# Splitting and moving small pieces around the attention of a two-layer decoder trunk, and cutting GpSimd's MLP tiles in halves

## The chip, the core and the metric

The kernel runs on one core of one Trainium2 chip. The metric is the device time of one execution, in microseconds. Five engines work side by side, each on its own list of instructions: PE multiplies matrices, DVE and ACT are the two wide elementwise engines, POOL (GpSimd) is a third, slower one, and SP issues the DMAs. PE's clock has two levels, 1.2 and 2.4 GHz; the profile shows it as a granted share, 0.50 and 1.00, and something between where a window holds both.

## What is computed

One sequence of 1024 tokens and width 1024 goes through two layers, all in float32:

```python
h = x
h = h + gla_mix(rmsnorm(h), ...)                  # layer 0: chunked gated linear attention, 4 heads
h = h + conv_ffn(rmsnorm(h), ...)                 # MLP0, hidden 2816, causal conv of width 3
k, v = shared_kv(h, ...)                          # one K/V projection, rotary on k
h = h + diff_attn(rmsnorm(h), k, v, ...)          # layer 1: 8 heads, 128 values each, causal
h = h + conv_ffn(rmsnorm(h), ...)                 # MLP1
return rmsnorm(h)

# diff_attn, per head: two score maps of 64 features each
a = softmax(q1 @ k1.T) - lam * softmax(q2 @ k2.T)
o = rmsnorm(a @ v) * (1 - lam_init)               # per head and token
# conv_ffn
u = h @ w_in ; c = conv3(u) ; a, g = split(c) ; out = (silu(g) * a) @ w_out
```

## The kernel before

Features lie on the 128 partitions and the 1024 tokens along a tile, in eight tiles of features. A float32 operand is split into a hi part (`xh`, `wh`, and the first half of `wp`, `xp`, `rp`, `lp`), which ACT copies with rounding, and a lo part (`xl`, `wl`, the second half), which is the operand less its hi part. A product is three matmuls, hi by hi, hi by lo, lo by hi. The lo part is mostly made by DVE (`lo_of`, a `scalar_tensor_tensor`, line 117), in some places by POOL (`tt`, line 114). `fine` (line 314) cuts an operation of 1024 columns on POOL into four of 256; on DVE it leaves it whole.

**The MLPs** use a scheme with seven products of half size in place of eight, so sums and differences of quarters are needed. Of the weights these are `sums`, `pieces` and `pieces_by_form` (lines 215 to 250): POOL makes them in 128x512 tiles, and `halves` (line 205) splits each result into `wp`. `mid` (line 855) adds the products (`u`) and `mix` (line 948) makes the sums of the hidden tiles (`c` to `mt`), both in part on POOL. `Wide.factor0` (line 401) scales a tile of the normalized stream and splits it with `halves` into `xp`; it is called eight times ahead of each MLP, half of them for the quarter "11", half for "21".

**Attention** (from line 1245) first projects and rotates. `rope_unit` (line 1260) projects k or q of a head for half of the tokens; after the second half it sends `xsb` through a DMA that swaps partitions, into `xw`. `rope_end` finishes the rotation in the next unit (`xw` by `sinr`, then `y` plus `xw`) and puts the rotated tile in a list, which the next call stores to DRAM, `kd` or `qd` (line 1253). `Attn.load` (line 1293) reads it again into `st`, and `qk_split` splits it. For head 0 the table `todo` (line 1477) names after which of the projection units this happens.

Then a loop runs over 64 steps (8 heads of 8 blocks of 128 queries), with the parts of several blocks in flight: scores (line 1332), maximum (`mx`), exponentials (`e`, line 1350), combination of both maps, transposes (`tp`, line 1378), hi and lo of the transposed weights (`ah` on ACT, `al` on DVE), and the products with v (`pv`, lines 1392 to 1394). A list `fill` hangs other work onto the steps: the projections of the later heads until step 46, the last `rope_end`, loads (`osr`) and splits of finished heads, loads of the residual `h`, and from step 48 on the units of the output product (`wo_unit`, line 1440, tile `dwo`). `finish` (line 1415) normalizes a head's output `osb`: PE spreads `ro` over the partitions (`rb`, line 311), DVE multiplies. The last head's output is split whole and completes the last W_o units. `wo_unit` adds to `h`, and `Late.add` sums the squares (`ssq`) that `begin` (line 389) multiplies by ones.

PE, ACT and SP run in the order in which the program is written. DVE's and POOL's order is made by a scheduler when the program is built.

Of the kernel before, what the change touches and what calls it, by code (L numbers as in the profile page):

```python
# [50 lines left out]
def trunk(  # L51
# [153 lines left out]
    def halves(x, name, eng=None):  # L205

        t = U(name, F32R)
        ACT.activation(t[:, H(0)], x, AF.Copy)  # L208
        if eng is POOL:
            tt(POOL, t[:, H(1)], x, t[:, H(0)].bitcast(F32), ALU.subtract)  # L210
        else:
            lo_of(DVE, t[:, H(1)], x, t[:, H(0)])
        return t

    def sums(ra, rg):

        tmp = U("wt")
        a11, a12, a21, a22 = ra[:, H(0)], ra[:, H(1)], rg[:, H(0)], rg[:, H(1)]
        s1, s2 = tmp[:, H(0)], tmp[:, H(1)]
        tt(POOL, s1, a21, a22, ALU.add)  # L220
        tt(POOL, s2, s1, a11, ALU.subtract)
        tt(POOL, a21, a11, a21, ALU.subtract)
        return a11, a12, a21, a22, s1, s2

    def pieces(ra, rg):


        a11, a12, s3, a22, s1, s2 = sums(ra, rg)
        yield halves(a11, "wp")
        yield halves(s2, "wp")  # L230
        tt(POOL, s2, a12, s2, ALU.subtract)
        yield halves(a12, "wp")
        yield halves(s3, "wp")
        yield halves(s1, "wp")
        yield halves(a22, "wp")
        pair.clear()
        yield halves(s2, "wp")

    def pieces_by_form(*raws):
# [6 lines left out]
        for a11, a12, s3, a22, s1, s2 in xs:  # L246
            tt(POOL, a12, a12, s2, ALU.subtract)
        for q in (1, 4, 5, 2, 3):
# [65 lines left out]
    def fine(eng, o, a, b, op):  # L314

        for c in range(0, 1024, 256 if eng is POOL else 1024):
            q = slice(c, c + 256 if eng is POOL else 1024)
            tt(eng, o[:, q], a[:, q], b[:, q], op)
# [46 lines left out]
    class Wide:  # L365
# [35 lines left out]
        def factor0(self, d):  # L401

            self.f["11" if d < ND // 2 else "21"].append(halves(self.scaled(d, 0), "xp"))

# [443 lines left out]
    def ffn(l, nm, g):  # L848
# [6 lines left out]
        def mid(i, n, o):  # L855
# [3 lines left out]
            if i < 2:  # L859
# [9 lines left out]
                elif n == 1:  # L869
                    tt(DVE, g1, o, g1, ALU.add)  # L870
                    tt(POOL, a2, a2, g1, ALU.add)
                elif n == 3:
                    tt(DVE, g1, o, g1, ALU.add)
                    tt(POOL, g2, g2, g1, ALU.add)
                else:
                    tt(DVE, g1, o, g1, ALU.add)
# [71 lines left out]
        def mix(i):  # L948
# [4 lines left out]
            t, u = U("mt"), U("mt")  # L953
            tt(POOL, t[:, H(0)], b12, b11, ALU.subtract)
            tt(POOL, t[:, H(1)], b22, t[:, H(0)], ALU.subtract)
            tt(POOL, b12, b22, b12, ALU.subtract)
            tt(POOL, u[:, H(0)], b21, t[:, H(1)], ALU.subtract)
            if i == NF - 1:
# [288 lines left out]

    rp, tails, stores = {}, deque(), deque()

    def rope_end(eng=None):  # L1250
# [3 lines left out]
        while tails:  # L1254
            dst, y, xw = tails.popleft()
            fine(eng, xw, xw, sinr, ALU.mult)
            fine(eng, y, y, xw, ALU.add)
            stores.append((dst, y))

# [20 lines left out]
    def kq_units(hh):  # L1280
        return [(rope_unit, dst, sc, hf, part) for dst, sc in ((kd[hh], 1.0), (qd[hh], HD ** -0.5))
                for hf in range(2) for part in range(2)]

    class Attn:
# [8 lines left out]
        def load(self, j):  # L1293

            r = rawtile("st")
            self.raw[j] = r
# [118 lines left out]
        def finish(self):  # L1415
            for hf in range(2):
                stt(DVE, self.osb[:, H(hf)], self.osb[:, H(hf)], sub_w, bcast_rows(self.ro, H(hf)), ALU.mult, ALU.mult)

    osp = [dram.tile([P, S], F32, name=f"osp{i}") for i in range(AH - 2)]
    h, on, wdo = {}, [], {}  # L1420
# [15 lines left out]

    def o_split():
        on.append(split(osr.popleft(), eng=OE))

    def wo_unit(g, d, hf, ks=range(4)):  # L1440
# [25 lines left out]
        if hf == 1:  # L1466
# [5 lines left out]
    steps = AH * NB  # L1472
    OE = POOL
    KQE, OL, OS, RS, WOB, RE = 46, 45, 46, 47, 48, DVE
    AHEAD, LOADS = 1, 2
    heads = {0: Attn(0)}
    todo = {0: [(heads[0].load, 2)], 6: [(heads[0].load, 1)], 9: [(heads[0].qk_split, 1), (heads[0].v_split,)],
            10: [(heads[0].load, 0)], 13: [(heads[0].qk_split, 0)]}
    SIDE = DVE
# [13 lines left out]

    spread([u for a in range(2, AH) for u in kq_units(a)], -2, KQE)
    fill[KQE + 1].append((rope_end, RE))
    fill[KQE + 1].append((rope_end,))
    spread([(o_load, q) for q in range(4)], OL, OL + 1)
    spread([(o_split,) for q in range(4)], OS, OS + 1)
    fill[RS] += [(residual, d) for d in DORD]
    spread([(o_load, q) for q in (4, 5)], steps - 4, steps - 3)  # L1500
    spread([(wo_unit, 0, d, hf) for d in DORD for hf in range(2)], WOB, steps - 1)

    for s in range(-2, steps + 5):
        a, i = divmod(s + 2, NB)
# [42 lines left out]
        if 0 <= s - 4 < steps:  # L1547
            b, j = divmod(s - 4, NB)
            if j == NB - 1:
                hd = heads.pop(b)  # L1550
                hd.finish()
                if b < AH - 2:
                    nc.sync.dma_start(osp[b], hd.osb)
                elif b == AH - 2:
                    last = [split(hd.osb, eng=POOL)]
                else:
                    last.append(split(hd.osb))
        if s == steps - 1:
# [4 lines left out]
        if steps <= s < steps + 3:  # L1563
            for d in DORD[2 * (s - steps):2 * (s - steps) + 2]:
                wo_unit(1, d, 0, range(3))
    on.append(last[1])
# [112 lines left out]
```

## Time and profile before

| | |
|---|---|
| median of three runs | 2384.3 us (2382.56 to 2384.98) |
| the profiled execution's own time | 2386.05 us |
| its span | 2384.3 us |
| PE busy | 2323.3 us (97%) |
| DVE busy | 1823.3 us (76%) |
| ACT busy | 1041.2 us (44%) |
| POOL busy | 710.2 us (30%) |

By the trace, MLP0 runs from about 447 to 1085 us, the first projections of the attention from 1200, its heads from 1240 to 1656, the last units of W_o to about 1703, and MLP1 follows. A row of a time-ordered view gives start, duration, engine, line, operation, the tile written and those read, the shape, and in brackets how long the engine stood idle before and what it waited for. Adjacent equal operations stand in one row with their count (x2); durations of pipelined rows overlap a little.

### The profile page before, as it was taken

What the parts mean: (1) busy time and instruction counts of PE and PEld (TensorE: products, weight loads), DVE (VectorE), ACT (ScalarE), POOL (GpSimd) and SP (SyncE); (2) the same over time, 40 slices, a digit from 0 to 9 for tenths busy, and PEclk for the clock granted to TensorE, in tenths of its full rate; (3) what the DMA queues carried; (4) which work ended last, traced back from release to release, by engine and by line L of the source; (5) the groups of instructions that cost most, each with busy time, mean ns of one, the idle gap of its engine ahead of it and who ended that gap; (6) DMA issues with size and microseconds to landing.
All of it is one profiled execution on the core that took longest, in us unless ns stands there. A gap on an engine that the chain in (4) does not pass through costs nothing. (4 is left out here: it accounts for less than half of the span.)

```text
span 2384.3 us, 29798 instructions
## 1 busy us (share of the span) xinstructions
PE 2323.3 (97%) x10954; PEld 1884.4 (79%) x10954; DVE 1823.3 (76%) x2605; ACT 1041.2 (44%) x1865; POOL 710.2 (30%) x718
## 2 busy tenths in 40 slices
PE   9999999999999999999999999899999999999997
PEld 7878887777888888888877888777767888888886
DVE  6554554799999999867147877666799999999865
ACT  5433352344333444544125555543353433344553
POOL 0210101055545430000005655622046544441001
PEclk9999999999999999999999999999999999999998
DMA  5012134122323347324243333512213323248423
GB/s 185 1 53 71 54 109 161 43 84 88 112 102 105 106 186 278 119 75 176 82 141 114 112 110 116 182 67 92 76 45 115 124 84 115 84 147 305 145 84 102
DMA packets 101427, 271.25 MB, mean 114 GB/s; under 512 B 10272, under 2 KB 23200, under 8 KB 101280
## 3 DMA queue, kind: packets, MB, share of 16 engines
q1 hardware_dynamic: 101280, 269.34, 33.6%
q8 instruction: 86, 1.41, 0.2%
q14 instruction: 61, 0.50, 0.1%
HBM read 184.89 MB, written 76.02 MB: 109 GB/s over the span
## 5 line engine op out<-in xcount | busy, mean ns | idle before, releaser
L908 PE MATMUL pf<-xp,wp 128*128 128x512 f32 x1232 | 488.8, 397 | 12.8 <-DVE wp L117 12.7
L907 PE MATMUL pf<-xp,wp 128*128 128x512 f32 x1232 | 488.3, 396 | 1.5 <-ACT xp L208 1.3
L909 PE MATMUL pf<-xp,wp 128*128 128x512 f32 x1232 | 487.8, 396 | 1.7 <-DVE xp L117 1.5
L908 PEld LDWEIGHTS pf<-xp,wp 128*128 128x128 f32 x1232 | 232.3, 189 | 73.3 <-DVE wp L117 19.5
L907 PEld LDWEIGHTS pf<-xp,wp 128*128 128x128 f32 x1232 | 232.1, 188 | 59.1 <-ACT xp L208 3.3
L909 PEld LDWEIGHTS pf<-xp,wp 128*128 128x128 f32 x1232 | 232.1, 188 | 59.0 <-DVE xp L117 5.5
L1016 PE MATMUL out<-rp,lp 128*128 128x512 f32 (+1 forms) x632 | 247.0, 391 | 1.5 <-ACT rp L208 1.5
L1018 PE MATMUL out<-rp,lp 128*128 128x512 f32 (+1 forms) x632 | 246.6, 390 | 0.0
L117 DVE SCALAR_TENSOR_TENSOR c<-u,cv,c 128x1024 f32<-128x1024 f32 x176 | 246.4, 1402 | 0.0
L1017 PE MATMUL out<-rp,lp 128*128 128x512 f32 (+1 forms) x632 | 246.2, 390 | 0.0
L117 DVE SCALAR_TENSOR_TENSOR wp<-raw,wp 128x512 fp32r<-128x512 f32 x180 | 202.7, 1135 | 13.5 <-ACT wp L208 13.2
L114 DVE TENSOR_TENSOR u<-pf,u 128x512 f32<-128x512 f32 x300 | 200.4, 680 | 15.1 <-PE pf L909 10.1
L278 PE MATMUL pf<-xh,wh 128*128 128x512 f32 x458 | 186.3, 407 | 1.1 <-ACT wh L198 1.1
L114 POOL TENSOR_TENSOR rs_y<-rs_m,nhalf 128x4 f32<-128x4 f32 (+2 forms) x26 | 31.4, 1207 | 517.0 <-DVE rs_m L294 487.0
L279 PE MATMUL pf<-xh,wl 128*128 128x512 f32 x458 | 181.1, 395 | 0.8 <-DVE wl L117 0.8
L280 PE MATMUL pf<-xl,wh 128*128 128x512 f32 x458 | 181.1, 395 | 0.0
L934 ACT ACTIVATE c<-c 128x1024 f32<-128x1024 f32 x44 | 46.7, 1062 | 268.4 <-DVE c L117 268.4
L117 DVE SCALAR_TENSOR_TENSOR wp<-wt,wp 128x512 fp32r<-128x512 f32 x128 | 150.4, 1176 | 2.5 <-ACT wp L208 2.5
L1016 PEld LDWEIGHTS out<-rp,lp 128*128 128x128 f32 x632 | 119.1, 188 | 28.5 <-ACT rp L208 1.9
L1018 PEld LDWEIGHTS out<-rp,lp 128*128 128x128 f32 x632 | 119.2, 189 | 27.6 <-DVE rp L117 0.8
L1017 PEld LDWEIGHTS out<-rp,lp 128*128 128x128 f32 x632 | 119.2, 189 | 26.8
L114 POOL TENSOR_TENSOR wt<-raw,wt 128x512 f32<-128x512 f32 x40 | 57.1, 1428 | 253.7 <-DVE wp L117 253.7
(251 smaller groups left out, 4977.8 us busy)
## 6 DMA issues: line engine op xcount, KB each, us to landing
raw<-in_w_in SPq DMA_DIRECT2D x88, 512.0 KB, 3.8
tr<-td SPq DMA_DIRECT2D x70, 512.0 KB, 4.1
td<-c SPq DMA_DIRECT2D x44, 512.0 KB, 2.8
wo<-in_w_out SPq DMA_DIRECT2D x44, 512.0 KB, 8.2
raw<-in_w_gla SPq DMA_DIRECT2D x24, 512.0 KB, 6.1
h<-hs SPq DMA_DIRECT2D x24, 512.0 KB, 4.8
td<-mt SPq DMA_DIRECT2D x22, 512.0 KB, 3.8
hs<-h SPq DMA_DIRECT2D x32, 256.0 KB, 2.0
```

Of the source, the lines that this page charges most:

```text
L114: eng.tensor_tensor(out=o, in0=a, in1=b, op=op)
L117: eng.scalar_tensor_tensor(out=o, in0=a, scalar=s, in1=b, op0=op0, op1=op1)
L278: PE.matmul(o, wh[:, k], xh[:, H(hf)], start=(k == 0), stop=False)
L279: PE.matmul(o, wl[:, k], xh[:, H(hf)], start=False, stop=False)
L280: PE.matmul(o, wh[:, k], xl[:, H(hf)], start=False, stop=(k == ND - 1))
L907: PE.matmul(o, wh, xh, start=(k == 0), stop=False)
L908: PE.matmul(o, wl, xh, start=False, stop=False)
L909: PE.matmul(o, wh, xl, start=False, stop=(k == ND // 2 - 1))
L934: ACT.activation(gt, gt, AF.Silu)
L1016: PE.matmul(o, wh, xh, start=(j == 0 or cut and j == NJ - LASTF), stop=False)
L1017: PE.matmul(o, wl, xh, start=False, stop=False)
L1018: PE.matmul(o, wh, xl, start=False, stop=(j == NJ - 1 or cut and j == NJ - LASTF - 1))
```

## The change

It has six parts.

1. POOL's 128x512 operations in `halves`, `sums`, `pieces`, `pieces_by_form`, `mid` and `mix` go through `fine`, which now takes any width: two operations of 256 columns each, 272 tiles in both MLPs.
2. In `factor0` the lo halves for "21" (four per MLP) are made by POOL instead of DVE.
3. The first head's rotated q and k are kept in SBUF (`kept`) and split from there; no store to `kd[0]`, `qd[0]` and no load from it. `todo` is changed to suit.
4. The last two calls of `rope_end` hang on steps 48 and 49 instead of both on 47.
5. The fourth of the first four `o_split` gives its lo part to DVE instead of POOL.
6. The last head's output is normalized and split by halves of 512 tokens (`finish_split`), ahead of the sixth of the units that need only the other three heads, instead of behind all of them.

```diff
 def halves(x, name, eng=None):
     if eng is POOL:
-            tt(POOL, t[:, H(1)], x, t[:, H(0)].bitcast(F32), ALU.subtract)
+            fine(POOL, t[:, H(1)], x, t[:, H(0)].bitcast(F32), ALU.subtract)
...
 def fine(eng, o, a, b, op):
-        for c in range(0, 1024, 256 if eng is POOL else 1024):
-            q = slice(c, c + 256 if eng is POOL else 1024)
+        n = o.shape[-1]
+        for c in range(0, n, 256 if eng is POOL else n):
+            q = slice(c, c + 256 if eng is POOL else n)
             tt(eng, o[:, q], a[:, q], b[:, q], op)
...
 def factor0(self, d):
-            self.f["11" if d < ND // 2 else "21"].append(halves(self.scaled(d, 0), "xp"))
+            q, eng = ("11", DVE) if d < ND // 2 else ("21", POOL)
+            self.f[q].append(halves(self.scaled(d, 0), "xp", eng))
...
 def rope_end(eng=None):
-            stores.append((dst, y))
+            if dst in (0, 1):
+                kept[dst] = y
+            else:
+                stores.append((dst, y))
...
 def load(self, j):
+            if self.hh == 0 and j < 2:
+                self.raw[j] = kept.pop(j)
+                return
...
+        def finish_split(self):
+            xh, xl = U("xh", F32R), U("xl", F32R)
+            for hf in range(2):
+                o = self.osb[:, H(hf)]
+                stt(DVE, o, o, sub_w, bcast_rows(self.ro, H(hf)), ALU.mult, ALU.mult)
+                ACT.activation(xh[:, H(hf)], o, AF.Copy)
+                lo_of(DVE, xl[:, H(hf)], o, xh[:, H(hf)])
+            return xh, xl
...
-    todo = {0: [(heads[0].load, 2)], 6: [(heads[0].load, 1)], 9: [(heads[0].qk_split, 1), (heads[0].v_split,)],
-            10: [(heads[0].load, 0)], 13: [(heads[0].qk_split, 0)]}
+    todo = {0: [(heads[0].load, 2)], 5: [(heads[0].load, 1), (heads[0].qk_split, 1)], 7: [(heads[0].v_split,)],
+            9: [(heads[0].load, 0)], 10: [(heads[0].qk_split, 0)]}
...
-    fill[KQE + 1].append((rope_end, RE))
-    fill[KQE + 1].append((rope_end,))
+    fill[KQE + 2].append((rope_end, RE))
+    fill[KQE + 3].append((rope_end,))
...
-    spread([(o_split,) for q in range(4)], OS, OS + 1)
+    spread([(o_split, (POOL, POOL, POOL, DVE)[q]) for q in range(4)], OS, OS + 1)
...
         if steps <= s < steps + 3:
-            for d in DORD[2 * (s - steps):2 * (s - steps) + 2]:
-                wo_unit(1, d, 0, range(3))
+            for u in range(2 * (s - steps), 2 * (s - steps) + 2):
+                if u == 5:
+                    last.append(heads.pop(AH - 1).finish_split())
+                wo_unit(1, DORD[u], 0, range(3))
```

At the end of the attention PE's list reads as follows; `dwo` are W_o units, `rb` spreads the last head's `ro`. Before:

```order
L1457 MATMUL dwo_14127<-xh_13998,wh_14077 128x512
L1458 MATMUL dwo_14127<-xh_13998,wl_14078 128x512
...
L1458 MATMUL dwo_14127<-xh_13765,wl_14078 128x512
L1459 MATMUL dwo_14127<-xl_13766,wh_14077 128x512
L311 MATMUL rb_14137<-ident,ro_14071 128x128 x4
L311 MATMUL rb_14143<-ident,ro_14071 128x128 x4
L1457 MATMUL dwo_14048<-xh_14149,wh_13828 128x512
```

After:

```order
L1476 MATMUL dwo_14248<-xh_13896,wl_14209 128x512
L1477 MATMUL dwo_14248<-xl_13897,wh_14208 128x512
L311 MATMUL rb_14260<-ident,ro_14202 128x128 x4
L311 MATMUL rb_14268<-ident,ro_14202 128x128 x4
L1475 MATMUL dwo_14276<-xh_14129,wh_14208 128x512
L1476 MATMUL dwo_14276<-xh_14129,wl_14209 128x512
L1477 MATMUL dwo_14276<-xl_14130,wh_14208 128x512
```

The nine matmuls of the sixth ready unit, which stood ahead of `rb`, now stand behind it.

On DVE, around the last rotation (`xw`, `y`) and the lo parts of the attention weights (`al`), before:

```order
L114 TENSOR_TENSOR y_12620<-y_12620,xw_12866 128x1024
L117 SCALAR_TENSOR_TENSOR al_12763<-tp_12898,ah_12761 128x4x128
L117 SCALAR_TENSOR_TENSOR al_12764<-tp_12905,ah_12762 128x4x128
...
L117 SCALAR_TENSOR_TENSOR e_12921<-e_12921,rc_13010 128x256
L117 SCALAR_TENSOR_TENSOR al_12917<-tp_13006,ah_12916 128x128
```

After:

```order
L114 TENSOR_TENSOR y_12754<-y_12754,xw_13000 128x1024
L117 SCALAR_TENSOR_TENSOR al_12897<-tp_13032,ah_12895 128x4x128
L117 SCALAR_TENSOR_TENSOR al_12898<-tp_13039,ah_12896 128x4x128
...
L117 SCALAR_TENSOR_TENSOR e_13055<-e_13055,rc_13138 128x256
L117 SCALAR_TENSOR_TENSOR xl_13074<-osr_13007,xh_13073 128x1024
L117 SCALAR_TENSOR_TENSOR al_13051<-tp_13134,ah_13050 128x128
```

The rotation keeps its place ahead of the two `al`; the fourth split's lo part (`xl` from `osr`) is new ahead of the next `al`.

On DVE, at the end of W_o (`xp` from `factor0`, `h` the last residual add, `ssq` the last square), before:

```order
L117 SCALAR_TENSOR_TENSOR xp_14414<-h_12961,xp_14414 128x512
L117 SCALAR_TENSOR_TENSOR xp_14418<-h_12963,xp_14418 128x512
L117 SCALAR_TENSOR_TENSOR wp_14421<-raw_14113,wp_14421 128x512
L117 SCALAR_TENSOR_TENSOR wp_14424<-raw_14109,wp_14424 128x512
L117 SCALAR_TENSOR_TENSOR wp_14427<-raw_14113,wp_14427 128x512
L114 TENSOR_TENSOR h_12963<-dwo_14430,h_12963 128x512
L114 TENSOR_TENSOR ssq_9199<-ssq_9199,sq_14445 128x512
```

After:

```order
L117 SCALAR_TENSOR_TENSOR xp_14556<-h_13089,xp_14556 128x512
L114 TENSOR_TENSOR h_13091<-dwo_14573,h_13091 128x512
L117 SCALAR_TENSOR_TENSOR wp_14564<-raw_14244,wp_14564 128x512
L117 SCALAR_TENSOR_TENSOR wp_14567<-raw_14240,wp_14567 128x512
L117 SCALAR_TENSOR_TENSOR wp_14570<-raw_14244,wp_14570 128x512
L114 TENSOR_TENSOR ssq_9339<-ssq_9339,sq_14588 128x512
```

One `xp` of each pair has gone to POOL, and the last residual add now stands ahead of the three `wp`.

## Rows read from the trace of the kernel before

**Rows 1.** Busy time of each engine, share of the span, instructions

```profile
PE 2323.3 (97%) x10954; PEld 1884.4 (79%) x10954; DVE 1823.3 (76%) x2605; ACT 1041.2 (44%) x1865; POOL 710.2 (30%) x718
```

**Rows 2.** PE's waits over the whole span: total us, times, longest us

```profile
PE pf L908 <- DVE wp L117: 12.7, 10, 2.0
PE pv L1394 <- DVE al L117: 8.9, 2, 5.0
PE st L389 <- DVE ssq L114: 4.2, 1, 4.2
...
PE dwo L1459 <- POOL xl L114: 0.9, 1, 0.9
```

**Rows 3.** Time-ordered rows of ACT, first head (start us, us, operation, idle before)

```profile
1239.90 1.06 ACT L323 ACTIVATE xh<-st 128x1024 fp32r<-128x1024 f32 x1 [4.20 <-DMA st<-qd]
```

**Rows 4.** Time-ordered rows of PE, first head

```profile
1241.02 0.38 PE L1332 MATMUL sp<-xh,xh 64*128 64x256 f32 x2 [0.69 <-ACT xh L323]
1242.28 0.38 PE L1332 MATMUL sp<-xh,xl 64*128 64x256 f32 x2 [0.88 <-DVE xl L117]
...
1248.79 0.33 PE L1378 MATMUL tp<-ident,e 128*128 128x128 f32 x1 [1.24 <-DVE e L117]
...
1258.20 0.60 PE L1332 MATMUL sp<-xh,xh 64*128 64x512 f32 x1 [1.77 <-ACT e L1350]
```

**Rows 5.** Time-ordered rows of DVE, first head

```profile
1241.00 1.23 DVE L117 SCALAR_TENSOR_TENSOR xl<-st,xh 128x1024 fp32r<-128x1024 f32 x1 [3.93 <-ACT xh L323]
...
1244.41 1.22 DVE L114 TENSOR_TENSOR xw<-xw,sinr 128x1024 f32<-128x1024 f32 x1
```

**Rows 6.** Windows: stretch, us, busy PE, PEld, DVE, ACT, POOL, granted clock, DMA share, GB/s

```profile
1257.00:1263.00 6.00, 4.80 (x26) 4.24 (x27) 4.49 (x6) 2.11 (x8) 2.20 (x2) 0.72 0.26 98
1660.00:1672.00 12.00, 9.90 (x23) 6.71 (x24) 7.16 (x10) 3.67 (x6) 0.00 (x0) 0.57 0.29 109
1704.00:1712.00 8.00, 4.37 (x14) 3.86 (x15) 4.72 (x11) 2.27 (x4) 3.95 (x7) 0.60 0.31 100
```

**Rows 7.** Time-ordered rows of DVE around the last rotation

```profile
1534.56 1.24 DVE L114 TENSOR_TENSOR xw<-xw,sinr 128x1024 f32<-128x1024 f32 x1 [1.04 <-DMA xw<-xsb]
...
1543.51 0.29 DVE L117 SCALAR_TENSOR_TENSOR al<-tp,ah 128x128 fp32r<-128x128 f32 x1 [3.50 <-ACT ah L1382]
```

**Rows 8.** Groups of DVE by line and shape (busy, mean ns, idle); then single POOL rows

```profile
L117 DVE SCALAR_TENSOR_TENSOR wp<-raw,wp 128x512 fp32r<-128x512 f32 x180 | 202.7, 1135 | 13.5 <-ACT wp L208 13.2
L114 DVE TENSOR_TENSOR u<-pf,u 128x512 f32<-128x512 f32 x300 | 200.4, 680 | 15.1 <-PE pf L909 10.1
...
612.24 1.29 POOL L114 TENSOR_TENSOR wt<-raw,wt 128x512 f32<-128x512 f32 x1 [6.01 <-DVE wp L117]
...
1326.80 2.81 POOL L114 TENSOR_TENSOR xl<-st,xh 128x256 fp32r<-128x256 f32 x4 [1.17 <-ACT xh L323]
```

**Rows 9.** Window in the middle of MLP1, columns as in rows 6

```profile
1850.00:1900.00 50.00, 50.00 (x217) 40.45 (x216) 50.00 (x52) 18.66 (x27) 25.21 (x20) 1.00 0.27 91
```

**Rows 10.** Time-ordered rows of PE, end of the last head

```profile
1655.78 0.40 PE L1459 MATMUL dwo<-xl,wh 128*128 128x512 f32 x1
1656.02 1.95 PE L311 MATMUL rb<-ident,ro 128*128 128x128 f32 x16
1659.96 0.50 PE L1457 MATMUL dwo<-xh,wh 128*128 128x512 f32 x1 [1.99 <-ACT xh L323]
...
1661.22 0.79 PE L1459 MATMUL dwo<-xl,wh 128*128 128x512 f32 x1 [0.53 <-DVE xl L117]
1662.80 0.80 PE L1457 MATMUL dwo<-xh,wh 128*128 128x512 f32 x1 [0.79 <-DVE h L114]
```

**Rows 11.** Time-ordered rows of DVE, end of the last head and of W_o

```profile
1652.09 0.17 DVE L114 TENSOR_TENSOR ro<-rs_y,rs_t 128x8 f32<-128x8 f32 x1
...
1701.58 1.29 DVE L117 SCALAR_TENSOR_TENSOR xp<-h,xp 128x512 fp32r<-128x512 f32 x2
...
1705.97 1.60 DVE L114 TENSOR_TENSOR ssq<-ssq,sq 128x512 f32<-128x512 f32 x1 [0.70 <-ACT sq L383]
```

More of the change, by code (lines that the diff above doesn't have):

```diff
@@ L219, in sums @@
         s1, s2 = tmp[:, H(0)], tmp[:, H(1)]
-        tt(POOL, s1, a21, a22, ALU.add)
-        tt(POOL, s2, s1, a11, ALU.subtract)
-        tt(POOL, a21, a11, a21, ALU.subtract)
+        fine(POOL, s1, a21, a22, ALU.add)
+        fine(POOL, s2, s1, a11, ALU.subtract)
+        fine(POOL, a21, a11, a21, ALU.subtract)
         return a11, a12, a21, a22, s1, s2
@@ L230, in pieces @@
         yield halves(s2, "wp")
-        tt(POOL, s2, a12, s2, ALU.subtract)
+        fine(POOL, s2, a12, s2, ALU.subtract)
         yield halves(a12, "wp")
@@ L246, in pieces_by_form @@
         for a11, a12, s3, a22, s1, s2 in xs:
-            tt(POOL, a12, a12, s2, ALU.subtract)
+            fine(POOL, a12, a12, s2, ALU.subtract)
         for q in (1, 4, 5, 2, 3):
@@ L870, in mid @@
                     tt(DVE, g1, o, g1, ALU.add)
-                    tt(POOL, a2, a2, g1, ALU.add)
+                    fine(POOL, a2, a2, g1, ALU.add)
                 elif n == 3:
                     tt(DVE, g1, o, g1, ALU.add)
-                    tt(POOL, g2, g2, g1, ALU.add)
+                    fine(POOL, g2, g2, g1, ALU.add)
                 else:
@@ L953, in mix @@
             t, u = U("mt"), U("mt")
[L954 to L957, printed above, removed]
+            fine(POOL, t[:, H(0)], b12, b11, ALU.subtract)
+            fine(POOL, t[:, H(1)], b22, t[:, H(0)], ALU.subtract)
+            fine(POOL, b12, b22, b12, ALU.subtract)
+            fine(POOL, u[:, H(0)], b21, t[:, H(1)], ALU.subtract)
             if i == NF - 1:
@@ L1246, in trunk @@
     tt(POOL, sinr, sinr, nkv.rbc, ALU.mult)
-    rp, tails, stores = {}, deque(), deque()
+    rp, tails, stores, kept = {}, deque(), deque(), {}
     def rope_end(eng=None):
@@ L1280, in kq_units @@
     def kq_units(hh):
-        return [(rope_unit, dst, sc, hf, part) for dst, sc in ((kd[hh], 1.0), (qd[hh], HD ** -0.5))
+        return [(rope_unit, dst, sc, hf, part) for dst, sc in ((kd[hh] if hh else 1, 1.0), (qd[hh] if hh else 0, HD ** -0.5))
                 for hf in range(2) for part in range(2)]
@@ L1435, in o_load, with o_split @@
         osr.append(t)
-    def o_split():
-        on.append(split(osr.popleft(), eng=OE))
+    def o_split(eng=POOL):
+        on.append(split(osr.popleft(), eng=eng))
     def wo_unit(g, d, hf, ks=range(4)):
@@ L1472, in trunk @@
     steps = AH * NB
-    OE = POOL
     KQE, OL, OS, RS, WOB, RE = 46, 45, 46, 47, 48, DVE
@@ L1501, in trunk @@
     spread([(wo_unit, 0, d, hf) for d in DORD for hf in range(2)], WOB, steps - 1)
-    for s in range(-2, steps + 5):
+    for s in range(-2, steps + 3):
         a, i = divmod(s + 2, NB)
@@ L1548, in trunk @@
             b, j = divmod(s - 4, NB)
-            if j == NB - 1:
+            if j == NB - 1 and b < AH - 1:
                 hd = heads.pop(b)
@@ L1553, in trunk @@
                     nc.sync.dma_start(osp[b], hd.osb)
-                elif b == AH - 2:
+                else:
                     last = [split(hd.osb, eng=POOL)]
-                else:
-                    last.append(split(hd.osb))
         if s == steps - 1:
```

## Prediction

> **What bounds the kernel now.** I read the busy shares first. PE works 2323.3 of 2384.3 us [rows 1], so 61 us are idle, and a change that removes no matmul can win only from these and from stretches in which PE runs below full clock. Next I read the list of PE's waits [rows 2]: the reader is to see that no wait is large (the first is 12.7 us in 10 pieces), that each has its place, and that edits of this change stand at several of them. Then I followed each place in the time-ordered rows of PE, ACT and DVE, and read the granted clock there from the windows. Last I looked at the MLPs, where POOL's tiles are cut: in a typical 50 us PE is busy 50.00 and DVE 50.00 at a clock of 1.00 [rows 9], so the MLP is PE's, with DVE close behind.
>
> The profiled execution took 2386.05 us, 1.75 above the median 2384.3 of the runs shown. The sum is made against 2386.05, and 1.75 is taken off at the end. About 0.2% (4.8 us) is what a measurement of this kernel can tell from no change.
>
> **First head's q and k kept in SBUF.** Four DMAs go: store and reload of k and of q. ACT's split of q stood 4.20 us for the reload and began only at 1239.90 [rows 3]; so the first scores waited 0.69 us for the hi half and 0.88 for the lo half [rows 4]. These 1.57 go for certain, since the rotated tile now stays in SBUF. DVE stood still 3.93 us ahead of that lo half, and did the next rotation only after it: xw at 1244.41 [rows 5], y behind it, then a weight's scaling, all three of some 1.2 us and all ahead of the e that the first transpose waits for. In the new order that rotation stands in what was idle, so 2.4 us go from before e, and with them the wait of 1.24 at 1248.79 [rows 4]. The wait of 1.77 at 1258.20 [rows 4] follows from the same late chain; I take 1.2 of it as gone, as DVE has other work there too. The clock was 0.72 on average in the 6 us around it, in which PE was busy 4.80 [rows 6]: 4.80 x 0.28 = 1.3 us of work lost, which I count as given back. Sum **-5.3**, between -1.6 (the certain part alone) and -5.9 (1.77 in place of 1.2). SP loses two waits for y and nothing is queued worse behind them; the two tiles are held longer, which costs no instruction.
>
> **Last rotation.** The table puts its two calls one and two steps later. But DVE's rows there keep their order: xw, y, the two al. PE's longest wait, 5.0 us for al [rows 2], comes from xw, which itself waits 1.04 us for a DMA [rows 7], and from y and al behind it. I cost this at **0**. What moves is SP's store of the rotated q: it stood ahead of the eight loads of h and held them until y was written; now it stands behind them. They start some 4 us sooner, on a queue that the loads of osr and of xw use at that moment; if xw's DMA suffers, the wait grows by about 1 us. If in time the rotation did leave al's way, the 5.0 would go. Bounds -5 and +1.
>
> **Fourth split of W_o's input on DVE.** POOL has four pieces less (2.81 us when nothing stands beside them [rows 8]) and DVE one operation of some 1.2 us more, ahead of an al before which DVE had 3.50 us without work [rows 7]. PE's only wait for that POOL queue is 0.9 [rows 2]; it goes: **-0.9**, at worst 0.
>
> **Last head's output by halves.** Before, PE did all ready W_o units, then rb, and stood while DVE scaled two halves, ACT copied and DVE subtracted: 1.99 us, then 0.53 [rows 10]. Now rb comes nine matmuls sooner, and these are left to do behind it. One takes 0.24 us (1655.78 to 1656.02 [rows 10]), nine 2.1. The chain from rb to the first product took 3.9 (1656.02 to 1659.96) for both halves at once; for the first half alone about half of it, 2.0, is covered. ro was ready at 1652.26 [rows 11], before rb's new place at 1653.9, so moving rb brings no wait. So 2.5 go. From 1660 to 1672 the clock was 0.57 on average and PE busy 9.90 [rows 6]: 9.90 x 0.43 = 4.3 us of work lost. The two waits of 0.79 for the residual add (one is shown [rows 10]) stay and could draw some of the slow stretch again; I take 0.9, a fifth, back. Sum **-5.9**, between -2.5 and -6.8.
>
> **Four lo halves from DVE to POOL, per MLP.** Ahead of MLP1 PE waits 4.2 us for the last sum of squares [rows 2]. On DVE's way to it stand four of the moved operations (a pair takes 1.29 [rows 11], so 0.6 each, 2.4). The last residual add now also stands ahead of three wp instead of behind them, so the sum no longer waits 0.70 for ACT [rows 11]. It would be reached 3.1 us sooner and a wait of about 1 remain. The sum itself took 1.60 instead of the 0.68 of such tiles, beside POOL's work [rows 11]; POOL's eight new pieces lie right here and can hold DVE some more, for which I take 1.0. From 1704 to 1712 the clock was 0.60 and PE busy 4.37 [rows 6], 1.7 us lost, which come back with the wait shorter. -3.1 - 1.7 + 1.0 is **-3.8**, between +1 (POOL's pieces take it all and more) and -5.9 (the whole 4.2 and 1.7). Ahead of MLP0 PE waits for nothing of the kind: 0.
>
> **POOL's 272 MLP tiles in halves.** A 128x512 tile takes 1.29 us, four 128x256 pieces 2.81, or 0.70 each [rows 8]: 0.12 more per tile, 33 us on an engine that works 30% of the span [rows 1]. That is hidden. What matters is DVE. An operation of DVE with two inputs in SBUF is held up beside POOL: wp takes 1135 ns on average, while u<-pf, of the same size with one input in PSUM, takes 680 [rows 8]; that is 0.455 x 180 = 82 us of holding in this group alone. A piece holds DVE half as long, but there are twice as many. The two about cancel, and PE has no wait in the MLP's middle to win: **0**. The ends are -8 (most of the 12.7 us of waits for wp [rows 2], which lie at the starts of both MLPs, go) and +20 (rival c).
>
> By the Trainium skill, page "SBUF — State Buffer", section "Who interferes with whom", the pair of ports that both engines use is locked by one of them for a whole instruction. The gap between 1135 and 680 agrees. By that rule the halves lock as long in all or longer, nothing is won for DVE, and the sum would have up to +20 in place of 0: this is rival (c).
>
> **Sum.** -5.3 + 0 - 0.9 - 5.9 - 3.8 + 0 = -15.9; 2386.05 - 15.9 - 1.75 = 2368.4, said as **2368**.
>
> **Rivals.**
> (a) The waits go, the clock doesn't come back, because other waits near by stay. For it: the two of 0.79 and the two for al. Against it: where PE has no wait the rows show 1.00 [rows 9]. Then 4.0 (first head: 1.57 + 1.24 + 1.2) + 0.9 + 1.6 (2.5 less 0.9) + 2.1 (3.1 less 1.0) = 8.6, and 2386.05 - 8.6 - 1.75 gives **2376**. Chance 0.15.
> (b) The pieces also serve DVE: one of them fits into the time of a u<-pf, which needs no second input from SBUF, where a whole tile of 1.29 sticks out beyond its 680 ns [rows 8]. Then the waits for wp shrink by 8 of 12.7 us: **2360**. Chance 0.15.
> (c) Slower, one mechanism: the halves hold DVE more. POOL works 33 us longer in the MLPs; if DVE is held for some 60% of that, since that share of its operations there reads two inputs from SBUF (I count wp and c against u), it has 20 us more to do, with 50.00 of 50 shown busy [rows 9]. If it has no reserve, PE waits as long: 2368 + 20 = **2388**. It decides from where PE shows waits for wp in the middle of MLP1, 1850 to 2300, where none are listed now. Against it: PE's waits end after the MLP's start, so DVE has a reserve. Chance 0.05.
> (d) The last rotation's move does take it out of al's way, in time if not in order: 2368 - 5 = **2363**. The rows' order is the same, so 0.05. Elsewhere, that the change doesn't do what it says is excluded by the order of PE and by the DMAs that are gone.
>
> **How the numbers follow.** The forecast has 0.60. Its small ends give 2386.05 - 1.6 - 0 - 2.5 - 0.5 - 1.75, near 2379.5 (I take 0.5 for the sum of squares, as all three failing together with +1 is not likely), its large ends 2386.05 - 5.9 - 0.9 - 6.8 - 5.9 - 1.75, near 2365. With (b) together with large ends the low end goes to 2357; with (a) the high end stays at 2379. Outside lie (c) and the failure of several terms at once. Faster by over 0.2% means below 2379.5: nearly all of the forecast, (a), (b) and (d), 0.86. Within 0.2%: 0.09. Slower: 0.05.
>
> **What would show it.** No wait of PE for the first head's q, none of 1.2 at the first transpose, and a clock near 1.00 from 1257 to 1263; no wait for xh behind rb, and no 10 us at half clock behind the attention; the wait for the last sum of squares about 1 instead of 4.2; the waits for al unchanged, one of 5.0 and one of about 4. wp at a mean near 1.1 us, PE at 50.00 in the MLP's middle. It is wrong if waits for wp appear there, if those at the MLPs' starts vanish, or if the slow clock stays where its wait has gone.

## The result, and the profile after

The changed kernel takes 2369.75 us (median of six runs, 2368.72 to 2372.4), the kernel before in the same comparison 2384.64: a ratio of 0.9941, with a 95% interval of 0.9932 to 0.9951. That is 14.9 us less; 2368 was forecast, with 2357 to 2379 as range. The profiled execution took 2368.72 us, its span is 2366.9.

The busy shares after answer to [rows 1]:

```profile
PE 2314.1 (98%) x10954; PEld 1874.5 (79%) x10954; DVE 1772.3 (75%) x2599; ACT 1042.9 (44%) x1866; POOL 852.4 (36%) x1002
```

PE is busy 9.2 us less with the same 10954 matmuls, so they ran at a higher clock on average; the windows below show where. DVE is busy 51 us less, POOL 142 us more. PE's waits, in answer to [rows 2]:

```profile
PE pf L910 <- DVE wp L117: 12.9, 12, 1.6
PE pv L1402 <- DVE al L117: 8.9, 2, 5.0
...
PE pf L909 <- ACT wp L208: 2.4, 1, 2.4
...
PE dwo L1477 <- DVE xl L117: 0.9, 1, 0.9
```

The waits for wp and for al are the same; the 4.2 for the last square is gone, and at the same place a new one of 2.4 stands, which the list puts down to ACT's copy of a weight; the rows below show that it is for DVE. The single wait for POOL's xl is gone as well; the 0.9 in the last row is another place (the last head's output).

**First head.** The time-ordered rows of PE, in answer to [rows 4], show no wait where there were three, and 0.24 where there was 1.77:

```profile
1238.09 0.38 PE L1340 MATMUL sp<-xh,xh 64*128 64x256 f32 x2
...
1243.48 0.33 PE L1386 MATMUL tp<-ident,e 128*128 128x128 f32 x1
...
1251.37 0.51 PE L1340 MATMUL sp<-xh,xh 64*128 64x512 f32 x1 [0.24 <-ACT e L1358]
```

DVE's rows, in answer to [rows 5], show the later rotation's xw ahead of the scores, in what had been idle, and its y right after:

```profile
1233.91 1.22 DVE L114 TENSOR_TENSOR xw<-xw,sinr 128x1024 f32<-128x1024 f32 x1
...
1239.43 1.22 DVE L114 TENSOR_TENSOR y<-y,xw 128x1024 f32<-128x1024 f32 x1
```

**Clock.** Windows of the changed kernel at the places of [rows 6] (first head, end of the last head, end of W_o) and of [rows 9]:

```profile
1246.00:1252.00 6.00, 5.76 (x32) 3.76 (x32) 4.65 (x9) 2.43 (x6) 5.99 (x8) 1.00 0.38 144
1646.00:1658.00 12.00, 9.55 (x39) 6.96 (x38) 10.63 (x14) 5.36 (x9) 2.77 (x4) 1.00 0.34 130
1684.00:1692.00 8.00, 5.59 (x19) 4.15 (x17) 6.04 (x9) 4.33 (x8) 6.30 (x11) 0.79 0.18 68
1850.00:1900.00 50.00, 50.00 (x217) 40.39 (x216) 48.19 (x52) 18.85 (x27) 34.13 (x39) 1.00 0.28 96
```

The first two stand at 1.00 (before: 0.72 and 0.57). In the second, 39 matmuls are done where there were 23. The third rose only to 0.79.

**End of the last head.** PE's rows, in answer to [rows 10]:

```profile
1643.98 1.95 PE L311 MATMUL rb<-ident,ro 128*128 128x128 f32 x16
1645.68 0.48 PE L1475 MATMUL dwo<-xh,wh 128*128 128x512 f32 x1
...
1649.37 0.50 PE L1477 MATMUL dwo<-xl,wh 128*128 128x512 f32 x1 [0.89 <-DVE xl L117]
1650.65 0.50 PE L1475 MATMUL dwo<-xh,wh 128*128 128x512 f32 x1 [0.79 <-DVE h L114]
```

After rb, PE goes on at once with the nine matmuls, and the wait for xh is gone. One for xl is still there, 0.89 us: DVE's two halves of xl took 3.29 us in place of the 1.23 of the whole one, beside POOL's MLP pieces, as the rows of DVE and POOL below show. This wait is not fixed by the program: of the nine kernels here that split the last head by halves (the changed one and those below that keep its sixth part) four show it and five do not (in one of these, `u4_rotation_as_before`, the same two halves took 2.41).

```profile
1646.63 3.29 DVE L117 SCALAR_TENSOR_TENSOR xl<-osb,xh 128x512 fp32r<-128x512 f32 x2
...
1645.93 1.45 POOL L114 TENSOR_TENSOR wt<-wt,raw 128x256 f32<-128x256 f32 x2
```

**End of W_o.** Time-ordered rows of PE, ACT and DVE, in answer to [rows 11]:

```profile
1687.47 0.61 PE L909 MATMUL pf<-xp,wp 128*128 128x512 f32 x1 [2.41 <-ACT wp L208]
...
1686.34 1.65 ACT L208 ACTIVATE wp<-raw 128x512 fp32r<-128x512 f32 x3
...
1676.50 1.25 DVE L117 SCALAR_TENSOR_TENSOR xp<-h,xp 128x512 fp32r<-128x512 f32 x1
...
1686.64 0.68 DVE L114 TENSOR_TENSOR h<-dwo,h 128x512 f32<-128x512 f32 x1
1687.24 2.42 DVE L117 SCALAR_TENSOR_TENSOR wp<-raw,wp 128x512 fp32r<-128x512 f32 x3
1689.59 1.21 DVE L114 TENSOR_TENSOR ssq<-ssq,sq 128x512 f32<-128x512 f32 x1
```

The row of PE names ACT's copy (wp), which ends just then, at 1687.47. But DVE's last residual add ends at 1687.32, and in all nine kernels with the halves PE's first product of MLP1 starts 0.15 us behind the end of this add, wherever ACT stands. So PE waits for the add. In the three kernels in which the last head's output is whole the same product does not wait at all; why the halves bring this wait isn't shown. DVE's xp takes 1.25 where one alone takes about 0.65.

Where the time came from is best read between landmarks, the starts of certain PE rows. The table is worked out from these starts, in us:

```
stretch of PE's list                          before    after   difference
start to first score of head 0               1241.02  1238.09      -2.93
  (of it the wait for q: 0.69)
first score to first W_o product              301.45   296.60      -4.85
to rb of the last head but one                 73.78    71.63      -2.15
to the sum of squares of the first half        65.80    60.11      -5.69
to the first product of MLP1's second part    468.07   466.56      -1.51
to the last rb of the final norm              226.11   226.55      +0.44
```

Of the first row, 0.7 belongs to the change; the rest lies in the first 350 us and in MLP0 and comes and goes between executions (kernels below with the same code there reach W_o's first product of layer 0 at 345.4 to 349.0). 0.7 + 4.85 + 2.15 + 5.69 + 1.51 is 14.9, as large as the difference of the medians. That the two agree so closely is partly chance: the two profiled executions differ by 17.3 us.

### The profile page after: what moved, and what is told of

The parts are those of the page before. It is cut to its first block, busy times and chain, and to the rows that moved or that the text cites. A ratio compares the mean times of both kernels' runs of the same rounds, so it can differ in the third digit from the quotient of the medians.

```text
span 2366.9 us, 30070 instructions
## 1 busy us (share of the span) xinstructions
PE 2314.1 (98%) x10954; PEld 1874.5 (79%) x10954; DVE 1772.3 (75%) x2599; ACT 1042.9 (44%) x1866; POOL 852.4 (36%) x1002
## 5 line engine op out<-in xcount | busy, mean ns | idle before, releaser
L117 DVE SCALAR_TENSOR_TENSOR c<-u,cv,c 128x1024 f32<-128x1024 f32 x176 | 253.1, 1440 | 5.2 <-ACT c L916 5.2
L114 DVE TENSOR_TENSOR u<-pf,u 128x512 f32<-128x512 f32 x300 | 200.8, 681 | 17.3 <-POOL u L114 9.3
L117 DVE SCALAR_TENSOR_TENSOR wp<-raw,wp 128x512 fp32r<-128x512 f32 x180 | 167.5, 940 | 51.9 <-ACT wp L208 51.9
L114 POOL TENSOR_TENSOR wt<-raw 128x256 f32<-128x256 f32 x88 | 99.8, 1152 | 107.7 <-ACT xp L208 58.1
L117 DVE SCALAR_TENSOR_TENSOR wp<-wt,wp 128x512 fp32r<-128x512 f32 x128 | 122.1, 955 | 7.4 <-ACT wp L208 7.4
```

Source lines behind the costliest of these rows:

```text
L114: eng.tensor_tensor(out=o, in0=a, in1=b, op=op)
L117: eng.scalar_tensor_tensor(out=o, in0=a, scalar=s, in1=b, op0=op0, op1=op1)
```

## The experiments

Each of the six parts was undone alone in the changed kernel. The medians of such kernels lie within a few us of one another and their intervals overlap in part, so the stretches of the table above serve as the second reading. They are, in us, for every run:

```
                       heads   to rb   to first  to MLP1's   median, us
                               head 6  squares   2nd part
before                 301.45  73.78   65.80     468.07      2384.64
after                  296.60  71.63   60.11     466.56      2369.75
u1_whole_tiles         297.01  72.14   59.46     468.72      2371.36
u3_first_head_dram     300.24  73.15   59.15     465.89      2375.33
u6_last_head_whole     296.86  71.68   65.44     467.12      2377.21
u2_factor_on_dve       296.97  71.71   60.13     469.53      2373.82
u4_rotation_as_before  297.03  71.74   59.05     465.88      2368.18
u5_split_on_pool       297.07  72.25   59.19     466.45      2369.85
p1_pieces_alone        300.32  73.76   65.69     468.04      2384.03
i2_weights_first       297.16  71.65   61.38     468.79      2374.42
i3_rotation_on_pool    290.99  87.71   62.78     466.03      2382.32
v3_splits_earlier      292.17  72.24   59.13     465.67      2363.36
```

Where the code is the same, the first two stretches mostly repeat within about 0.6 us, the third and fourth within about 1. Four differ by more, by PE's clock: the first between the kernel before and `p1_pieces_alone` (1.1), the second of `u3_first_head_dram` (1.5), and the third of `i2_weights_first` (1.3) and `i3_rotation_on_pool` (2.7).

**First head through DRAM again.**

```diff
-            if dst in (0, 1):
-                kept[dst] = y
-            else:
-                stores.append((dst, y))
+            stores.append((dst, y))
...
-            if self.hh == 0 and j < 2:
-                self.raw[j] = kept.pop(j)
-                return
...
-    todo = {0: [(heads[0].load, 2)], 5: [(heads[0].load, 1), (heads[0].qk_split, 1)], 7: [(heads[0].v_split,)],
-            9: [(heads[0].load, 0)], 10: [(heads[0].qk_split, 0)]}
+    todo = {0: [(heads[0].load, 2)], 6: [(heads[0].load, 1)], 9: [(heads[0].qk_split, 1), (heads[0].v_split,)],
+            10: [(heads[0].load, 0)], 13: [(heads[0].qk_split, 0)]}
```

> The changed kernel with the first head's q and k through DRAM again. If this part is worth the 5.3 us forecast: 2375 us, PE waits of 0.7 and 0.9 for the first scores, 1.2 at the first transpose, 1.8 at the fourth or fifth scores, and a window of half clock there. If the waits only move: 2371 us.

2375.33 us (ratio to before 0.9957, 0.9945 to 0.9970), 5.6 more than the changed kernel. Three of the four waits are back, as PE's rows show; the one at the transpose is not:

```profile
1242.90 0.39 PE L1334 MATMUL sp<-xh,xh 64*128 64x256 f32 x2 [0.64 <-ACT xh L324]
1244.16 0.39 PE L1334 MATMUL sp<-xh,xl 64*128 64x256 f32 x2 [0.88 <-DVE xl L117]
1260.28 0.49 PE L1334 MATMUL sp<-xh,xh 64*128 64x512 f32 x1 [1.75 <-ACT e L1352]
```

In place of the wait at the transpose stands work at a lower clock: PE is busy without a gap in the 6 us around it, at 0.78, and the window that showed 0.72 before is at 1.00.

```profile
1246.00:1252.00 6.00, 6.00 (x26) 4.35 (x26) 5.83 (x11) 2.59 (x8) 0.00 (x0) 0.78 0.38 124
1257.00:1263.00 6.00, 4.25 (x30) 3.21 (x29) 5.93 (x9) 1.83 (x6) 4.29 (x5) 1.00 0.17 68
```

In their own place these are worth 3.64 (300.24 less 296.60) and 0.64, 4.3 in all; the stretch behind is 1.5 longer too, by the clock behind the second wait for al (below). The median's 5.6 agrees with the forecast of 5.3, and the waits did not merely move, which would have given 2371.

**The last head's output whole again.**

```diff
-            if j == NB - 1 and b < AH - 1:
+            if j == NB - 1:
...
-                else:
+                elif b == AH - 2:
                     last = [split(hd.osb, eng=POOL)]
+                else:
+                    last.append(split(hd.osb))
...
-                if u == 5:
-                    last.append(heads.pop(AH - 1).finish_split())
```

> The changed kernel with the last head's output normalized and split whole, behind all ready units. If the part is worth the 5.9 us forecast: 2375.5 us, PE waits 2.0 for xh and 0.5 for xl and runs at half clock for some 10 us behind. If DVE at the end of W_o would have made up for it (it is busy there in any case): 2372.

2377.21 us (0.9968, 0.9955 to 0.9980), 7.5 more. The third stretch is 5.3 longer, the fourth 0.6. The waits of before are back, and the clock behind them is 0.59 (PE's rows, then the window):

```profile
1652.16 0.50 PE L1475 MATMUL dwo<-xh,wh 128*128 128x512 f32 x1 [1.99 <-ACT xh L324]
1653.42 0.79 PE L1477 MATMUL dwo<-xl,wh 128*128 128x512 f32 x1 [0.40 <-DVE xl L117]
```

```profile
1653.00:1665.00 12.00, 10.03 (x27) 7.17 (x27) 7.06 (x11) 4.31 (x7) 0.00 (x0) 0.59 0.33 125
```

These 2.4 us of waits stand in place of the 0.89 for xl, so 1.5 more are waited, and 10.03 us of PE's work at 0.59 lose 10.03 x 0.41 = 4.1: together 5.6, near the 5.3 of the stretch. DVE at the end of W_o did not make up for it (2372 us would have shown that). The 0.6 of the fourth stretch is within what it repeats by.

**All lo halves of factor0 on DVE again.**

```diff
-            q, eng = ("11", DVE) if d < ND // 2 else ("21", POOL)
+            q, eng = "11" if d < ND // 2 else "21", DVE
```

> The changed kernel with all lo halves of factor0 on DVE again. Forecast for this part: 3.8 us, so 2373.5 us, with a wait of about 4 us for the last square. Rival, from the two profiles (the wait of 4.2 for the square became one of 2.4 for a weight's copy): the part is worth some 1.5 us, so 2371, because POOL's pieces hold DVE's own xp (1.25 us in place of 0.68) next to them.

2373.82 us (0.9955, 0.9942 to 0.9969), 4.1 more; 3.0 in the fourth stretch. PE waits 4.76 us ahead of MLP1 instead of 2.4, by the list too for DVE's last residual add, which now stands behind the three wp again:

```profile
1690.68 0.69 DVE L114 TENSOR_TENSOR h<-dwo,h 128x512 f32<-128x512 f32 x1
...
1691.51 0.77 PE L909 MATMUL pf<-xp,wp 128*128 128x512 f32 x1 [4.76 <-DVE h L114]
```

Taken out of the changed kernel, the part is thus worth about what was forecast (3.8), and not the 1.5 of the rival. But from before to after the same stretch gained only 1.5. With the last head whole the stretch is 467.12 with the move, and 468.07 in the kernel before without it: only 1.0. The rows of `u6_last_head_whole` show why the move is worth less there: PE's first product does not wait for the last add (it starts before the add), PE waits for the last square as in the kernel before, and this wait fell only from 4.18 to 2.98:

```profile
1692.40 0.39 PE L909 MATMUL pf<-xp,wp 128*128 128x512 f32 x1
...
1694.14 0.69 DVE L114 TENSOR_TENSOR h<-dwo,h 128x512 f32<-128x512 f32 x1
...
1698.35 1.05 PE L390 MATMUL st<-ones,ssq 128*128 128x1 f32 x8 [2.98 <-DVE ssq L114]
```

Counted from the start of the first half's sum of squares, the move brings the end of the last square from 25.5 to 24.4 us, with the last head whole or by halves; the end of the last add it brings from 23.25 to 20.9. So what the move is worth depends on which of the two PE waits for: the square with the last head whole, the add with the halves.

**MLP weights first.** This asks whether the new wait of 2.4 is due to ACT's order, as the list of waits says.

```diff
-            if hf == 1 and u == ND - 1:
+            if hf == 1 and u == ND - 2:
                 prefetch(PF[1])
```

> The changed kernel with MLP1's first weights split one W_o unit sooner in program order, so that ACT copies them ahead of its last copies for factor0; DVE's order stays as it is. If ACT's order makes the wait of 2.4 us ahead of MLP1: the wait goes and with it the half clock, 2366 us. If DVE, which is busy without a gap there, is the bound: the same time within 1 us, and the wait is now for DVE's lo half of the same weights or for the last square.

2374.42 us (0.9954, 0.9941 to 0.9968): slower by 4.7, which neither had said. Of this 2.2 lie in the fourth stretch, where the edit works; the 1.3 of the third are PE's clock behind the same waits (last section). DVE's order did not stay: the lo halves of the three weights now run ahead of the last residual add, and the wait that PE shows in the list of waits is for that add:

```profile
PE pf L909 <- DVE h L114: 4.9, 1, 4.9
```

ACT's copies came sooner and PE did not: its first product starts again 0.15 us behind the last add. ACT's order was not the cause in the changed kernel either. The end of W_o is DVE's, and work put ahead of the last add is paid by PE.

**POOL's tiles whole in the changed kernel, and cut alone in the kernel before.**

```diff
         n = o.shape[-1]
-        for c in range(0, n, 256 if eng is POOL else n):
-            q = slice(c, c + 256 if eng is POOL else n)
+        w = 256 if eng is POOL and n > 512 else n
+        for c in range(0, n, w):
+            q = slice(c, c + w)
```

> The changed kernel with POOL's 128x512 tiles whole again (the four lo halves of factor0 stay on POOL, whole too). If cutting them is worth nothing, as forecast: 2369 to 2372 us, waits of PE for wp in all about 12.7 us as in both kernels, though DVE's busy time goes from 1772 back to about 1815 us. If the pieces serve DVE and PE gets some of that (rival b): 2374 us or more and more waits for wp. If the pieces cost (rival c): 2367 or less.

2371.36 us (0.9946, 0.9933 to 0.9958): 1.6 more than the changed kernel, within the spread. The waits for wp are 12.6 in all and DVE's busy time is 1825.0. The loss lies in the fourth stretch (2.2 longer), and there the rows of DVE and POOL tell why: the last add ends 22.0 us behind the start of the first half's sum, 1.1 later than in the changed kernel. DVE's own xp beside a whole tile of POOL takes 1.79, while in the kernel that makes all of them on DVE a pair takes 1.29 (the second fence):

```profile
1676.73 1.79 DVE L117 SCALAR_TENSOR_TENSOR xp<-h,xp 128x512 fp32r<-128x512 f32 x1
...
1676.69 1.29 POOL L114 TENSOR_TENSOR xp<-h,xp 128x512 fp32r<-128x512 f32 x1 [7.78 <-ACT xp L208]
```

```profile
1678.18 1.29 DVE L117 SCALAR_TENSOR_TENSOR xp<-h,xp 128x512 fp32r<-128x512 f32 x2
```

In the changed kernel, beside two pieces, the same operation takes 1.25. So handing a lo half to POOL whole costs DVE more than making it, and in pieces it is about even, where the two engines meet; it pays where they don't.

The cut alone, in the kernel before, is the diff of part 1 of the change and nothing else:

> The kernel before with POOL's 272 MLP tiles cut in halves and nothing else. Theory: 2384 to 2386 us, DVE's busy time down by some 45 us, POOL's up by some 130, PE's waits for wp in all the same within 1 us. Rival (b): 2380 or less with fewer waits for wp. Rival (c): 2388 or more.

2384.03 us, ratio 0.9999 (0.9990 to 1.0007): nothing, as forecast. Its busy shares, PE's first wait and a group of DVE:

```profile
PE 2322.3 (97%) x10954; PEld 1882.0 (79%) x10954; DVE 1774.6 (74%) x2605; ACT 1042.5 (44%) x1865; POOL 843.3 (35%) x990
```

```profile
PE pf L909 <- DVE wp L117: 12.6, 13, 1.6
```

```profile
L117 DVE SCALAR_TENSOR_TENSOR wp<-raw,wp 128x512 fp32r<-128x512 f32 x180 | 167.8, 941 | 49.6 <-ACT wp L208 49.6
```

DVE is busy 49 us less, POOL 133 more, and PE waits as long as before. wp takes 941 ns on average where it took 1135, but its idle time before it, waiting for ACT's copy, rose from 13.5 to 49.6: DVE finishes sooner and then stands. The MLP is PE's.

**The last rotation and the fourth split.** Each undone alone, with one run of each kernel:

```diff
-    fill[KQE + 2].append((rope_end, RE))
-    fill[KQE + 3].append((rope_end,))
+    fill[KQE + 1].append((rope_end, RE))
+    fill[KQE + 1].append((rope_end,))
```

> The changed kernel with the last two calls of rope_end at the step where they were. Forecast for this part 0: the wait of 5.0 for al as it is, from al 1 to the first W_o unit the same length within 0.3 us; only the loads of h start later on SP.

The wait for al, which stands in the first stretch, is 4.96 against 4.97. From it to the first W_o product 4.92 us pass against 4.40, a little more than the 0.3 allowed, at a lower clock (0.69 against 0.77 in the 8 us from the end of the wait). The first stretch is 297.03 against 296.60, the second 71.74 against 71.63, and the run took 2368.18: no gain or loss that can be told from none.

```diff
-    spread([(o_split, (POOL, POOL, POOL, DVE)[q]) for q in range(4)], OS, OS + 1)
+    spread([(o_split, (POOL, POOL, POOL, POOL)[q]) for q in range(4)], OS, OS + 1)
```

> The changed kernel with the fourth split of W_o's input on POOL again. Forecast for this part 0.9 us: PE waits 0.9 for POOL's xl at the fourth product of the first W_o unit, and nothing else moves.

The run took 2369.85. The wait is back, but only 0.35 us of it, and the second stretch is 0.6 longer:

```profile
1540.98 0.50 PE L1477 MATMUL dwo<-xl,wh 128*128 128x512 f32 x1 [0.35 <-POOL xl L114]
```

The second stretch fell by 2.15, of which 0.9 is that wait. Most of the rest is the clock behind the second wait for al, of 3.94 to 3.96 us in every run. The 8 us behind it, before and after:

```profile
1556.84:1564.84 8.00, 8.00 (x38) 6.51 (x38) 5.12 (x11) 3.63 (x8) 3.04 (x5) 0.66 0.01 2
```

```profile
1547.97:1555.97 8.00, 8.00 (x42) 6.60 (x43) 6.15 (x12) 4.35 (x10) 2.97 (x5) 0.80 0.04 13
```

0.14 of 8 us is 1.1. The 8 us behind this wait show 0.62 to 0.69 in the three kernels with the first head through DRAM (among them `u3_first_head_dram`, whose code is the changed one's there), 0.79 to 0.80 in seven with the first head in SBUF, and 0.65 and 0.71 in the two kernels below that move the rotation. In these traces, one of each kernel, the 1.1 thus goes with the first head's part; by what path, some 300 us later, stays open.

**The rotation out of al's way.** The change's fourth part did not do that, so two kernels try it in another way. The first gives the rotation to POOL:

```diff
-    KQE, OL, OS, RS, WOB, RE = 46, 45, 46, 47, 48, DVE
+    KQE, OL, OS, RS, WOB, RE = 46, 45, 46, 47, 48, POOL
```

> The changed kernel with the last rotation (xw, y) on POOL instead of DVE, so that it no longer stands ahead of the two al on DVE. If PE's wait of 5.0 us for al is due to DVE's xw (with its wait for a DMA) and y: about 1 us of it remains, the half clock behind it goes too (2.9 us of work), so 2363 us. Rival: POOL, which makes the lo halves of W_o's input there, falls behind by the eight pieces, and PE waits for these instead: 2367 to 2370.

2382.32 us (0.9984, 0.9975 to 0.9993), 12.6 more than the changed kernel. The wait for al fell to 1.01, and the first stretch by 5.6, as the theory had it; but three waits for POOL's xl came, 10.6 us in all, more than the rival had said, and the second stretch is 16 longer:

```profile
1526.93 0.38 PE L1402 MATMUL pv<-al,xh 128*128 128x256 f32 x1 [1.01 <-DVE al L117]
...
1544.00 0.79 PE L1477 MATMUL dwo<-xl,wh 128*128 128x512 f32 x1 [5.47 <-POOL xl L114]
```

The second makes the splits of W_o's input two steps sooner, and the scheduler then puts the rotation behind the two al by itself:

```diff
-    KQE, OL, OS, RS, WOB, RE = 46, 45, 46, 47, 48, DVE
+    KQE, OL, OS, RS, WOB, RE = 46, 43, 44, 47, 48, DVE
```

> The changed kernel with the four loads and splits of W_o's input two steps earlier (OL, OS = 43, 44); the last rotation stays on DVE, and in this build's order it then stands behind the two al instead of ahead of them. If PE's wait of 5.0 us is due to DVE's place for xw and y, as the prediction said: about 1 us of it remains, no window at half clock there, no wait for POOL's xl, so 2363 us. Rival: ACT's and POOL's earlier splits come beside the scores of head 5 and PE waits there for e or for al: 2368 or more.

2363.36 us (0.9911, 0.9895 to 0.9926): faster than both kernels, 6.4 less than the changed one, as expected. Of this 4.4 lie in the first stretch, where the wait is, and the second is 0.6 longer; the rest lies in the third and fourth, which other kernels with the same code show as short. What the rival feared came in small: PE's waits for e are 3.6 in all in place of 2.5. The wait for al is 0.70 (PE's row), because al comes at 1528.38 and xw only at 1533.15 (DVE's rows):

```profile
1529.11 0.38 PE L1402 MATMUL pv<-al,xh 128*128 128x256 f32 x1 [0.70 <-DVE al L117]
```

```profile
1528.38 1.27 DVE L117 SCALAR_TENSOR_TENSOR al<-tp,ah 128x512 fp32r<-128x512 f32 x2
...
1533.15 1.43 DVE L114 TENSOR_TENSOR xw<-xw,sinr 128x1024 f32<-128x1024 f32 x1
```

The second wait for al, 3.95 us, stays there too: DVE's chain for a head's norm waits 1.76 for POOL and stands ahead of it. Whether that chain makes the wait is not shown; no run changes it.

## Why the prediction was right, point by point

**First head, -5.3.** Right: 0.7 + 4.85 = 5.5 between the landmarks, all four waits gone or at 0.24, and the clock at 1.00. Undone, 5.6 came back in the median, of which 4.3 in its place. The wait of 1.24 at the transpose, which the sum took off, is no fixed cost of the old way: two other kernels with the first head through DRAM do not have it, one of them (`u3_first_head_dram`) with slower work in its place.

**Last rotation, 0.** Right, for the reason given: DVE's order was the same and so was the wait of 5.0. That the wait comes from xw's and y's place, the kernel with the splits earlier shows: with both behind al it fell to 0.70, and the first stretch lost 4.4 us. The range's end of -5 for this was right in size.

**Fourth split, -0.9.** The wait went; undoing the part brought only 0.35 of it back, so how much of it was this part's is not separated.

**Last head by halves, -5.9.** Right in size (5.69; undone 5.3 in its stretch), with two things not foreseen. DVE's xl stood beside POOL's pieces and a wait of 0.89 for it came, at a clock of 1.00. The deduction of 0.9 for the clock was not needed; that it was as large as this wait is luck. And with the halves PE waits ahead of MLP1 for the last residual add, a wait on no list of the kernel before.

**factor0, -3.8.** This is the term that failed in size: the stretch gained 1.5 (1.6 to 2.4 by five other kernels with the same code in it). The prediction had the last square reached 3.1 us sooner less 1.0 for POOL's hold, and PE waiting for it with about 1 left. The square came 1.2 sooner, not 2.1. The 1.0 was right: xp took 1.25 and 1.23 where POOL worked beside it, so four moved operations gave 1.3 of their 2.4. But the 0.70 of waiting for ACT did not go, it moved to the square before (0.76), and the three wp took 2.42 in place of 1.89 beside POOL; the square itself won 0.4, 1.21 in place of 1.60. And with the halves PE no longer waited for the square but, 2.41, for the last add, and the clock in the window rose only from 0.60 to 0.79. The third and fourth stretches together are 533.87 before, 532.56 with the move but the last head whole, 529.66 with the halves but not the move, and 526.67 with both: the move is worth 1.3 in the first pair and 3.0 in the second.

**Tiles in halves, 0.** Right in time (0.9999 alone), wrong in its working. That the two effects cancel is not so: wp is held far less. And POOL did not become 33 us busier but 133 (the cut alone): its pieces take longer beside DVE, 1.055 us on average for those of `raw` where the prediction took 0.70. It is hidden all the same. What rival (b) expected, that DVE is held less, is thus real (by the way it named, pieces beside u<-pf, is not shown), and its price nothing: DVE's gain turns into waiting for ACT, and PE's waits for wp are 12.6 us with the cut alone, 12.7 before. Rival (c) is excluded. The Trainium skill's rule of a lock for a whole instruction ("SBUF — State Buffer", "Who interferes with whom") agrees with the single rows, 1.79 beside a tile of 1.29 and 1.25 beside pieces; what was read from it in the prediction, that nothing would be won for DVE, does not.

**Sum.** -15.9 was forecast; the medians show 14.9. The sum came out nearer than its terms: factor0 brought about 2 us less than forecast, and the second stretch 1.1 more, by a clock that no term counted.

**Rivals (a) and (d).** The clock came back with the waits in the first head and behind the last; only ahead of MLP1, where a wait of 2.4 stays, it remained low (0.79 in the window). (d) did not happen.

## What to carry to other kernels

A wait on the critical engine is worth its own length and the low clock behind it: here 1.5 us more of waits cost 5.3 behind the last head, while three of 0.78 to 0.89 cost no clock in two kernels and some in two others. But two edits in a row don't simply add up: the first can change what PE waits for behind it, and the second is worth what it brings to that event, here 2.4 us for the last add and 1.2 for the last square. When a list of waits names an engine, look at whether another one's operation ended just before: a fixed distance between its end and the start, over several kernels, tells which it is. And where a scheduler sets an engine's order, move the work that it puts first (here the splits), not the call that one wishes to see later, and read the order that results.

## What the runs showed of the hardware that was not expected

Groups of DVE and POOL of the changed kernel, whose counterparts are in [rows 8] for the first two; POOL's `raw<-raw,raw` had a mean of 1780 ns for 44 whole tiles:

```profile
L114 DVE TENSOR_TENSOR u<-pf,u 128x512 f32<-128x512 f32 x300 | 200.8, 681 | 17.3 <-POOL u L114 9.3 <-PE pf L911 6.6
L117 DVE SCALAR_TENSOR_TENSOR wp<-raw,wp 128x512 fp32r<-128x512 f32 x180 | 167.5, 940 | 51.9 <-ACT wp L208 51.9
...
L114 POOL TENSOR_TENSOR raw<-raw,raw 128x256 f32<-128x256 f32 x88 | 91.2, 1055 | 0.0
```

Cutting POOL's operations in two moved the holding from one engine to the other: DVE's operation of two SBUF inputs fell from 1135 to 940 ns, while POOL's tile rose from 1.78 to 2 x 1.055 = 2.11 us. DVE's operation with one input in PSUM kept its 680.

What a wait costs in clock isn't told by its length. Behind the last head waits of 1.99 and 0.53 were followed by a clock of 0.57 over 12 us. Four kernels have three short ones there instead, of 0.89, 0.79 and 0.78 us or within 0.01 of it, on the same list of PE. In two of them, the changed kernel and `u2_factor_on_dve`, the clock stayed at 1.00; in the two others it fell, at a cost of 1.3 and 2.7 us in the third stretch. The 10 us from 40 us behind that stretch's start, in the changed kernel, `i2_weights_first` and `i3_rotation_on_pool`:

```profile
1646.32:1656.32 10.00, 7.55 (x31) 5.31 (x30) 8.84 (x12) 3.85 (x7) 2.44 (x4) 1.00 0.24 92
1650.02:1660.02 10.00, 7.55 (x25) 5.05 (x24) 7.57 (x10) 2.70 (x5) 2.45 (x4) 0.83 0.21 79
1657.36:1667.36 10.00, 7.54 (x23) 5.05 (x22) 7.62 (x9) 2.89 (x6) 2.42 (x4) 0.76 0.21 79
```

What sets it stays open.
